# A two-layer decoder trunk on one core: the 512-column products of every dense layer in parts of 256 columns

## The chip, the cores and the metric

The kernel runs on one core of one Trainium2 chip. The metric is the device time of one execution in microseconds. The kernel before takes 604.91 us (median of 3 runs, 603.92 to 605.07).

## The reference, cut to what matters

Two decoder layers (DEPTH = 2) over 256 tokens of width 1024. Each layer is a token mixer and a squared-ReLU MLP, each followed by a residual and a LayerNorm. Layer 0 mixes with stick-breaking attention, layer 1 with block attention, which for 256 tokens is plain causal softmax attention with rotary positions. All inputs are float32.

```python
for i in range(DEPTH):
    h = layer_norm(DEEPNORM_ALPHA * h + mixers[i](h), ln1_g, ln1_b)
    h = layer_norm(DEEPNORM_ALPHA * h + squared_relu_mlp(h, w1, w2), ln2_g, ln2_b)

def stick_breaking_attention(x, w_qkv, w_o):     # block attention has the same two products
    q, k, v = (split_heads(t, SB_HEADS) for t in jnp.split(x @ w_qkv, 3, axis=-1))
    ...
    return merge_blocks(o) @ w_o

def squared_relu_mlp(x, w1, w2):                 # w1 is 1024 x 4096, w2 is 4096 x 1024
    return jnp.square(jax.nn.relu(x @ w1)) @ w2
```

## The kernel before

**Dense products.** Every float32 operand is split into a high part (rounded to the type that TensorE takes at full rate) and a low rest: ScalarE rounds (line 205, `hi`), VectorE subtracts (line 206, `lo`). A product x·w is then three matmuls: high·high, high·low, low·high, all added into one PSUM bank. Weights come by DMA in units of 128 partitions x 4 x 512 (1 MB), are split on chip in halves of 1024 columns, and live in 5 pairs of buffers (`hi`, `lo`).

There are two forms. In `projT` (lines 329 to 349) the weights are the stationary operand and the 256 tokens are the moving one: its matmuls have 256 columns. It makes Q and K of layer 0 (`qkT_ps`) and the hidden layer of the MLP from its third block on (`up_ps` with `xh` or `xl` named first). In `mm3` (lines 193 to 197) the 128 tokens of one half t are stationary and the weights move: its matmuls have 512 columns, a whole bank. `mm3` makes V (`v_ps`), Q and K of layer 1 (`qk_ps`), the output projection (`wo_ps`), the first two hidden blocks of each MLP (`up_ps` with `hi` or `lo` named first, by `up_tok`) and the MLP's second product (`dn_ps`, by `down`). In the trace a name like `dn_ps<-hi,hh` gives the output, the moving operand (weights, `hi` or `lo`) and the stationary one (`hh` or `hl`, high and low of the hidden layer). Every matmul has a weight load of its own (LDWEIGHTS, engine PEld), also where two in a row have the same stationary operand.

**The MLP.** In each layer `up` and `down` alternate: 96 matmuls of 256 columns, then 48 of 512. The last product of the last layer alone already has one bank in two halves (`down`, line 678): 24 matmuls of `dn_ps` with 256 columns.

**The order.** A planner (`Plan`) builds the program. TensorE's dense matmuls are written in a fixed order; attention pieces, transposes, splits and loads are put in where the planner's own clocks say that their inputs are there (`poll` and `wait`). `mm3` advances the planner's TensorE clock by 3 x (0.006 + 0.000435 x columns), 0.686 for 512 columns. So a change of this number can move pieces on all engines. Attention pieces: `qkT` or `qk`, then (layer 1) rotary products on VectorE and an addition on GpSimd (line 543), transposes `tp`, scores `sc` (14 matmuls), softmax or stick-breaking on ScalarE and VectorE, transposes `pt_ps`, a copy (line 498), the product with V `o`.

After each LayerNorm the new x is transposed on TensorE (`xt`), split by ScalarE and VectorE into `xh` and `xl`, and used by the next dense product.

Of the kernel before, what the change touches and what calls it, by code (L numbers as in the profile page):

```python
# [154 lines left out]
def trunk(ctx: ExitStack, tc: tile.TileContext, x, xt, cst, cstb, w, ln, out):  # L155
# [17 lines left out]
    clock = plan.clock  # L173

    def abank(name):
        return acc.tile([P, 512], F32, tag="acc", name=name)
# [13 lines left out]
    def mm(ps, sta, mov, start, stop):  # L190
        nc.tensor.matmul(ps, sta, mov, start=start, stop=stop)  # L191

    def mm3(ps, sh, sl, wh, wl, start, stop):
        mm(ps, sh, wh, start, False)
        mm(ps, sh, wl, False, False)
        mm(ps, sl, wh, False, stop)
        clock["pe"] += 3 * (0.006 + 0.000435 * ps.shape[-1])

    def here():
        return Tok("pe", clock["pe"], 0.2)  # L200
# [24 lines left out]
    def tok(t):  # L225
        return slice(t * P, (t + 1) * P)
# [46 lines left out]
    def retire(n):  # L273
        plan.give([("split", n)], clock["pe"])
# [47 lines left out]
    def proj(t, us, ps):  # L322
        for k in range(KT):
            u = us[k // 4]
            plan.wait([u.tok[k % 4], XT[t][k]])
            mm3(ps, xh[:, k, tok(t)], xl[:, k, tok(t)], u.hi[:, k % 4, :], u.lo[:, k % 4, :], k == 0, k == KT - 1)
        plan.poll()
# [84 lines left out]
    for l in range(DEPTH):  # L412
# [162 lines left out]
        for kind in seq:  # L575
            us = take(2)
            j = int(kind[1])
            if kind[0] == "V":
                for t in range(NT):
                    plan.wait(take=[("acc", 1)])  # L580
                    ps = abank("v_ps")
# [14 lines left out]
        def wo(t, half):  # L596
            oh, ol = OT[half]
            us = (wo0, wo1)[half]
            ready = []
            for n in range(2):  # L600
                for k in range(4):
                    plan.wait([us[n].tok[k], mixed[2 * half + k // 2, k % 2]])
                    mm3(banks[t][n], oh[:, k, tok(t)], ol[:, k, tok(t)], us[n].hi[:, k, :], us[n].lo[:, k, :],
                        half == 0 and k == 0, half == 1 and k == 3)
                ready.append([(0, 512, here())])
            return ready
# [63 lines left out]
        def down(c, t, us):  # L670
            last = c == NFC - 1
            ready = [[], []]
            if not last:
                loop = [(n, k, 0, 512) for k in range(4) for n in range(2)]
            elif l < DEPTH - 1 or t == 0:
                loop = [(n, k, 0, 512) for n in range(2) for k in range(4)]
            else:
                loop = [(n, k, c0, c1) for n, c0, c1 in ((0, 0, 512), (1, 0, 256), (1, 256, 512)) for k in range(4)]
            for n, k, c0, c1 in loop:
                plan.wait([us[n].tok[k], HR[c][t][k]])  # L680
                hh, hl = HT[c]
                mm3(dn[t][n][:, c0:c1], hh[:, k, tok(t)], hl[:, k, tok(t)], us[n].hi[:, k, c0:c1], us[n].lo[:, k, c0:c1],
                    c == 0 and k == 0, last and k == 3 and c1 == 512)
                if k == 3:
                    ready[n].append((c0, c1, here()))
            if t == 1:
                plan.give([("st", 1)], clock["pe"])
                retire(2)
            return ready
# [8 lines left out]
        for c in range(2, NFC):  # L698
            us = take(2)
            up(c, us)  # L700
            retire(2)
            if c == 2:
                plan.wait(take=[("acc", 4)])
                dn = [[abank("dn_ps") for _ in range(2)] for _ in range(NT)]
            us = take(2)
            for t in range(NT):
                down(c - 2, t, us)
        d6, d7 = take(2), take(2)
        ended = []
        for t in range(NT):  # L710
            down(NFC - 2, t, d6)
            r = down(NFC - 1, t, d7)
            end = norm(t, dn[t], r, g2, to_x if l < DEPTH - 1 else to_out, base[t])
            base[t] = end[-1]
            ended += end
# [93 lines left out]
```

## Time and profile before

| | |
|---|---|
| median of 3 runs | 604.91 us (603.92 to 605.07) |
| the profiled execution | 603.84 us |
| its span, first to last instruction | 602.1 us |
| mean granted TensorE clock | 0.995 |
| TensorE matmuls busy | 591.5 us, 98% of the span, 3652 matmuls |
| weight loads busy | 507.1 us, 84% |
| VectorE, ScalarE, GpSimd busy | 389.7, 290.5, 24.6 us |
| DMA | 49% of 16 engines, 109 MB |

How to read it: a matmul's recorded duration (0.28 us for 256 columns, 0.39 us for 512) includes its way through a pipeline and overlaps with the next one. What a matmul costs in a stream is the distance from its start to the next start. That distance, called pace below, is read from the first and the last start of a run of matmuls and their count. The long chain of work through the program lies on TensorE for 95% of the span. The rest of the span is about 8.9 us of loading at its start and 8.2 us of LayerNorm and output at its end.

### The profile page before, as it was taken

What the parts mean: (1) busy time and instruction counts of PE and PEld (TensorE: products, weight loads), DVE (VectorE), ACT (ScalarE), POOL (GpSimd) and SP (SyncE); (2) the same over time, 40 slices, a digit from 0 to 9 for tenths busy, and PEclk for the clock granted to TensorE, in tenths of its full rate; (3) what the DMA queues carried; (4) which work ended last, traced back from release to release, by engine and by line L of the source; (5) the groups of instructions that cost most, each with busy time, mean ns of one, the idle gap of its engine ahead of it and who ended that gap; (6) DMA issues with size and microseconds to landing.
All of it is one profiled execution on the core that took longest, in us unless ns stands there. A gap on an engine that the chain in (4) does not pass through costs nothing.

```text
span 602.1 us, 8790 instructions
## 1 busy us (share of the span) xinstructions
PE 591.5 (98%) x3652; PEld 507.1 (84%) x3652; DVE 389.7 (65%) x492; ACT 290.5 (48%) x419; POOL 24.6 (4%) x30
## 2 busy tenths in 40 slices
PE   8999999999999999999999999999999999999994
PEld 6899987879899899898877777778798998899883
DVE  5877874878455554655879787668667537446454
ACT  5866663436443543642536655626346426435400
POOL 0000000000000000000122022000000000000000
PEclk9999999999999999999999999999999999999998
DMA  8994335185546337337274443443764464365101
GB/s 310 393 334 143 126 154 200 70 277 169 215 179 269 149 143 279 140 144 275 71 249 170 145 144 132 140 141 101 249 260 162 149 270 169 157 235 209 72 0 70
DMA packets 17895, 109.31 MB, mean 182 GB/s; under 512 B 1984, under 2 KB 2624, under 8 KB 5824
## 3 DMA queue, kind: packets, MB, share of 16 engines
q1 hardware_dynamic: 17856, 108.76, 49.0%
q8 instruction: 28, 0.46, 0.3%
q14 instruction: 11, 0.09, 0.0%
HBM read 107.71 MB, written 1.05 MB: 181 GB/s over the span
## 4 chain that ended last, share of the span: by engine, by line
PE 95%; DVE 2%; ACT 1%; DMA 1%; SPq 0%; issue 0%; DVEq 0%; ACTq 0%
PE dn_ps L191 29%; PE up_ps L191 28%; PE wo_ps L191 7%; PE v_ps L191 7%; PE qk_ps L191 7%; PE qkT_ps L191 7%; PE sc L191 3%; PE o L509 2%; PE xt L387 1%; PE tp L556 1%; DMA h<-in_xt 1%; DVE lo L206 1%; DVE xl L206 1%; PE ht_ps L663 1%; PE pt_ps L491 1%; PE pt_ps L493 1%
## 5 line engine op out<-in xcount | busy, mean ns | idle before, releaser
L206 DVE TENSOR_TENSOR lo<-raw,hi 128x1024 fp32r<-128x1024 f32 (+1 forms) x196 | 229.7, 1213 | 48.8 <-ACT hi L205 47.1
L205 ACT CAST hi<-raw 128x1024 fp32r<-128x1024 f32 (+1 forms) x196 | 192.0, 1032 | 64.2 <-issue 42.4
L191 PE MATMUL up_ps<-xh,hi 128*128 128x256 f32 x384 | 106.4, 277 | 0.0
L191 PE MATMUL up_ps<-xl,hi 128*128 128x256 f32 x384 | 106.2, 276 | 0.0
L191 PE MATMUL up_ps<-xh,lo 128*128 128x256 f32 x384 | 106.1, 276 | 0.0
L191 PE MATMUL dn_ps<-hi,hl 128*128 128x512 f32 (+1 forms) x260 | 101.5, 390 | 0.0
L191 PE MATMUL dn_ps<-lo,hh 128*128 128x512 f32 (+1 forms) x260 | 101.0, 388 | 0.0
L191 PE MATMUL dn_ps<-hi,hh 128*128 128x512 f32 (+1 forms) x260 | 100.2, 385 | 0.0
L191 PEld LDWEIGHTS up_ps<-xl,hi 128*128 128x128 f32 x384 | 72.1, 188 | 0.5
L191 PEld LDWEIGHTS up_ps<-xh,hi 128*128 128x128 f32 x384 | 72.1, 188 | 0.5
L630 DVE SCALAR_TENSOR_TENSOR r<-up_ps,r 128x512 f32<-128x512 f32 x32 | 22.0, 688 | 78.0 <-ACT r L628 78.0
L191 PEld LDWEIGHTS up_ps<-xh,lo 128*128 128x128 f32 x384 | 72.2, 188 | 0.0
L628 ACT ACTIVATE r<-up_ps 128x512 f32<-128x512 f32 x32 | 19.1, 596 | 95.0 <-PE up_ps L191 95.0
L191 PEld LDWEIGHTS dn_ps<-lo,hh 128*128 128x128 f32 x260 | 48.8, 188 | 10.5
L191 PEld LDWEIGHTS dn_ps<-hi,hh 128*128 128x128 f32 x260 | 48.8, 188 | 10.0
L191 PEld LDWEIGHTS dn_ps<-hi,hl 128*128 128x128 f32 x260 | 48.9, 188 | 9.4
L191 PE MATMUL qkT_ps<-xh,hi 128*128 128x256 f32 x128 | 36.8, 287 | 0.0
L191 PE MATMUL qkT_ps<-xh,lo 128*128 128x256 f32 x128 | 35.8, 280 | 0.2 <-DVE lo L206 0.2
L191 PE MATMUL qkT_ps<-xl,hi 128*128 128x256 f32 x128 | 35.7, 279 | 0.0
L205 ACT CAST xh<-xt 128x512 fp32r<-128x512 f32 x12 | 7.0, 587 | 42.9 <-PE xt L387 41.1
L191 PE MATMUL v_ps<-hi,xh 128*128 128x512 f32 x64 | 26.4, 413 | 0.0
L191 PE MATMUL qk_ps<-hi,xh 128*128 128x512 f32 x64 | 26.3, 411 | 0.0
(97 smaller groups left out, 885.8 us busy)
## 6 DMA issues: line engine op xcount, KB each, us to landing
raw<-in_w SPq DMA_DIRECT2D x64, 1024.0 KB, 5.0
raw<-in_wqkv SPq DMA_DIRECT2D x22, 1024.0 KB, 5.2
raw<-in_wo SPq DMA_DIRECT2D x8, 1024.0 KB, 4.8
raw<-in_first SPq DMA_DIRECT2D x8, 256.0 KB, 4.8
gb<-in_l_ln_g SPq DMA_DIRECT2D x4, 512.0 KB, 4.0
gb<-in_l_ln_b SPq DMA_DIRECT2D x4, 512.0 KB, 5.8
h<-in_x SPq DMA_DIRECT2D x2, 512.0 KB, 7.7
h<-in_xt SPq DMA_DIRECT2D x3, 256.0 KB, 4.8
```

The costliest lines, as they stand in the source:

```text
L191: nc.tensor.matmul(ps, sta, mov, start=start, stop=stop)
L205: f = lambda: nc.scalar.copy(hi(), src())
L206: g = lambda: nc.vector.tensor_tensor(lo(), src(), hi().bitcast(F32), op=ALU.subtract)
L387: nc.tensor.transpose(XB[t][:, n, k * P:(k + 1) * P], h[t][:, (4 * n + k) * P:(4 * n + k + 1) * P], ident)
L491: nc.tensor.transpose(ps[:, j, 0:P], pj[:, T:T + P], ident)
L493: nc.tensor.transpose(ps[:, j, T:T + P], pj[:, P:T], ident)
L509: nc.tensor.matmul(o[HD * j:HD * j + HD, 0, kt * P:T], v[kt][:, hd * HD:(hd + 1) * HD], pt[:, 0:T] if kt == 0 else pt[:, T:T + P], start=k ...
L556: nc.tensor.transpose(tb["tp"][:, pr, c0:c0 + P], QK[g, t]["qk"][:, e * T + pr * P:e * T + pr * P + P], ident)
L628: nc.scalar.activation(box["r", n], ps, AF.Relu)
L630: return dve(512, lambda: nc.vector.scalar_tensor_tensor(box["r", n], ps, 0.0, box["r", n], op0=ALU.max, op1=ALU.mult), after=[a], rank=0. ...
L663: nc.tensor.transpose(box["ht"][:, 0, k * P:(k + 1) * P], box["r", 0][:, k * P:(k + 1) * P], ident)
```

## The change

`mm3` cuts its columns into parts and runs the three matmuls of one part before those of the next. A part has 256 columns, with one exception: in the last block of `down` in each layer, for the first token half and the second bank, the parts have 384 and 128 columns. The planner's TensorE clock now advances per part by 3 x max(0.113, 0.000435 x columns): 0.678 for 512 columns in two parts of 256, 0.840 for 384 and 128.

```diff
-    def mm3(ps, sh, sl, wh, wl, start, stop):
-        mm(ps, sh, wh, start, False)
-        mm(ps, sh, wl, False, False)
-        mm(ps, sl, wh, False, stop)
-        clock["pe"] += 3 * (0.006 + 0.000435 * ps.shape[-1])
+    def mm3(ps, sh, sl, wh, wl, start, stop, cut=256):
+        n = ps.shape[-1]
+        parts = [slice(a, min(a + cut, n)) for a in range(0, n, cut)]
+        for i, c in enumerate(parts):
+            mm(ps[:, c], sh, wh[:, c], start and i == 0, False)
+            mm(ps[:, c], sh, wl[:, c], False, False)
+            mm(ps[:, c], sl, wh[:, c], False, stop and i == len(parts) - 1)
+            clock["pe"] += 3 * max(0.113, 0.000435 * (c.stop - c.start))
...
                 mm3(dn[t][n][:, c0:c1], hh[:, k, tok(t)], hl[:, k, tok(t)], us[n].hi[:, k, c0:c1], us[n].lo[:, k, c0:c1],
-                    c == 0 and k == 0, last and k == 3 and c1 == 512)
+                    c == 0 and k == 0, last and k == 3 and c1 == 512, 384 if last and t == 0 and n == 1 else 256)
```

On TensorE, at the start of the first `down` of layer 0 (`hi_1445` and `hi_1479` are the weights of the two banks; numbers are buffer names). Before:

```order
L191 MATMUL dn_ps<-hi_1445,hh 128x512
L191 MATMUL dn_ps<-lo_1446,hh 128x512
L191 MATMUL dn_ps<-hi_1445,hl 128x512
L191 MATMUL dn_ps<-hi_1479,hh 128x512
L191 MATMUL dn_ps<-lo_1480,hh 128x512
L191 MATMUL dn_ps<-hi_1479,hl 128x512
```

The same place on TensorE with the change:

```order
L191 MATMUL dn_ps<-hi_1721,hh 128x256
L191 MATMUL dn_ps<-lo_1722,hh 128x256
L191 MATMUL dn_ps<-hi_1721,hl 128x256
L191 MATMUL dn_ps<-hi_1721,hh 128x256
L191 MATMUL dn_ps<-lo_1722,hh 128x256
L191 MATMUL dn_ps<-hi_1721,hl 128x256
L191 MATMUL dn_ps<-hi_1767,hh 128x256
```

Each triple of 512 columns has become two triples of 256; a low weight (`lo`) is asked for after one matmul of 256 columns, not after one of 512.

On TensorE, in the last `down` of layer 0, first token half, where the first bank ends and the second begins, with the change:

```order
L191 MATMUL dn_ps<-lo_3124,hh 128x256
L191 MATMUL dn_ps<-hi_3123,hl 128x256
L191 MATMUL dn_ps<-hi_3200,hh 128x384
L191 MATMUL dn_ps<-lo_3201,hh 128x384
L191 MATMUL dn_ps<-hi_3200,hl 128x384
L191 MATMUL dn_ps<-hi_3200,hh 128x128
L191 MATMUL dn_ps<-lo_3201,hh 128x128
L191 MATMUL dn_ps<-hi_3200,hl 128x128
```

In this bank each of the 4 steps of its loop has three matmuls of 384 and three of 128 columns, where before it had three of 512; so 12 matmuls of 512 per layer, 24 in all, become 24 of 384 and 24 of 128.

On VectorE, in layer 1 behind the first three rotary products (`qk`, `rot`): `lo` is a weight split, `qkl` the split of a transposed head pair, `sma` the row maxima of scores. Before:

```order
L206 TENSOR_TENSOR lo_2909<-raw_2845,hi_2908 128x1024 x2
L206 TENSOR_TENSOR lo_2928<-raw_2871,hi_2927 128x1024
L206 TENSOR_TENSOR qkl<-tp,qkh 128x512
L206 TENSOR_TENSOR lo_2928<-raw_2871,hi_2927 128x1024
L533 TENSOR_TENSOR qk<-qk_ps,const 128x512
L465 TENSOR_REDUCE sma<-sc 128x2 x2
L468 TENSOR_SCALAR sma<-sma 128x4
L538 TENSOR_TENSOR rot<-qk_ps,const 128x512
L206 TENSOR_TENSOR qkl<-tp,qkh 128x512
```

The same place on VectorE with the change (three lines further down in the file):

```order
L209 TENSOR_TENSOR lo_3656<-raw_3553,hi_3655 128x1024 x2
L209 TENSOR_TENSOR lo_3684<-raw_3594,hi_3683 128x1024 x2
L536 TENSOR_TENSOR qk<-qk_ps,const 128x512
L541 TENSOR_TENSOR rot<-qk_ps,const 128x512
L209 TENSOR_TENSOR qkl<-tp,qkh 128x512 x2
L209 TENSOR_TENSOR lo_3747<-raw_3653,hi_3746 128x1024 x2
L468 TENSOR_REDUCE sma<-sc 128x2 x2
L471 TENSOR_SCALAR sma<-sma 128x4
L209 TENSOR_TENSOR qkl<-tp,qkh 128x512 x2
```

The fourth rotary product now stands ahead of the first head pair's split and its first scores; from here to the output projection of layer 1 the attention pieces stand in another order on TensorE, ScalarE and VectorE. In layer 0's attention a few pieces move by one or two steps of the loop, in the MLPs none.

## Rows read from the trace of the kernel before

**Rows 1.** The page: busy time of each engine; granted TensorE clock in 40 slices

```profile
PE 591.5 (98%) x3652; PEld 507.1 (84%) x3652; DVE 389.7 (65%) x492; ACT 290.5 (48%) x419; POOL 24.6 (4%) x30
...
PEclk9999999999999999999999999999999999999998
```

**Rows 2.** Waits of TensorE: line waited for, us in total, times, longest

```profile
PE warm_ps L285 <- POOL keep L451: 1.3, 1, 1.3
...
PE qk_ps L191 <- DVE lo L206: 0.2, 1, 0.2
```

**Rows 3.** Groups by form, TensorE: output, operands, shapes, count | busy, mean ns

```profile
L191 PE MATMUL dn_ps<-hi,hl 128*128 128x512 f32 x252 | 99.3, 394 | 0.0
...
L191 PE MATMUL v_ps<-hi,xh 128*128 128x512 f32 x64 | 26.4, 413 | 0.0
```

**Rows 4.** Timeline of TensorE, last `down`: start us, us, line, operands

```profile
560.81 0.39 PE L191 MATMUL dn_ps<-hi,hh 128*128 128x512 f32 x1
...
590.79 0.39 PE L191 MATMUL dn_ps<-hi,hl 128*128 128x512 f32 x1
591.02 0.28 PE L191 MATMUL dn_ps<-hi,hh 128*128 128x256 f32 x1
...
593.63 0.28 PE L191 MATMUL dn_ps<-hi,hl 128*128 128x256 f32 x1
```

**Rows 5.** Timeline of TensorE, one `up` block: its start, its seventh, its end

```profile
164.69 0.28 PE L191 MATMUL up_ps<-xh,hi 128*128 128x256 f32 x1
...
165.40 0.28 PE L191 MATMUL up_ps<-xh,hi 128*128 128x256 f32 x1
...
175.49 0.28 PE L191 MATMUL up_ps<-xh,lo 128*128 128x256 f32 x1
```

**Rows 6.** Timeline of TensorE, three runs of `qkT` in layer 0's attention

```profile
35.94 0.28 PE L191 MATMUL qkT_ps<-xl,hi 128*128 128x256 f32 x1
...
45.59 0.28 PE L191 MATMUL qkT_ps<-xh,lo 128*128 128x256 f32 x1
...
52.92 0.28 PE L191 MATMUL qkT_ps<-xl,hi 128*128 128x256 f32 x1
...
55.16 0.28 PE L191 MATMUL qkT_ps<-xh,lo 128*128 128x256 f32 x1
...
59.76 0.28 PE L191 MATMUL qkT_ps<-xl,hi 128*128 128x256 f32 x1
...
62.25 0.28 PE L191 MATMUL qkT_ps<-xh,lo 128*128 128x256 f32 x1
```

**Rows 7.** Stretches: us, busy of PE, PEld, DVE, ACT, POOL, clock, DMA, GB/s

```profile
35.94:45.59 9.65, 9.65 (x83) 9.65 (x83) 6.86 (x8) 5.23 (x7) 0.00 (x0) 1.00 0.94 336
165.40:175.49 10.09, 10.09 (x92) 10.09 (x90) 4.57 (x4) 2.76 (x3) 0.00 (x0) 1.00 0.72 274
297.40:397.40 100.00, 99.47 (x577) 76.96 (x576) 78.73 (x135) 57.13 (x123) 16.30 (x9) 1.00 0.49 169
```

**Rows 8.** Timeline of TensorE: transposes of 128 columns, and scores of 128 columns

```profile
394.12 0.27 PE L491 MATMUL pt_ps<-const,p 128*128 128x128 f32 x1
...
395.32 0.27 PE L493 MATMUL pt_ps<-const,p 128*128 128x128 f32 x1
...
76.84 0.23 PE L191 MATMUL sc<-qkh 64*128 64x128 f32 x2
76.89 0.29 PE L191 MATMUL sc<-qkl,qkh 64*128 64x128 f32 x2
77.01 0.28 PE L191 MATMUL sc<-qkh,qkl 64*128 64x128 f32 x2
```

**Rows 9.** Timeline of TensorE where `up` of layer 0 waits for a low weight

```profile
128.12 0.39 PE L191 MATMUL up_ps<-hi,xh 128*128 128x512 f32 x1
128.65 0.51 PE L191 MATMUL up_ps<-lo,xh 128*128 128x512 f32 x1
```

**Rows 10.** Timeline of GpSimd in layer 1's attention: a rotary addition

```profile
316.90 2.12 POOL L543 TENSOR_TENSOR qk<-qk,rot 128x512 f32<-128x512 f32 x1 [2.67 <-DVE rot L538]
```

## The prediction

> **What bounds the kernel now.** [...] The groups by form give the counts: dn_ps has three groups of 252 matmuls with 512 columns, and v_ps, qk_ps, wo_ps and the first up_ps have three of 64 each [rows 3]. That is 756 + 4 x 192 = 1524 matmuls with 512 columns, all of which the change cuts. 24 go to 384 and 128 columns, 1500 to two parts of 256.
>
> **Paces before.** 512 columns: 132 dn_ps matmuls start from 560.81 to 590.79, 29.98 / 131 = 228.85 ns [rows 4]. 256 columns of the very same product: 24 from 591.02 to 593.63, 2.61 / 23 = 113.5 ns [rows 4]. An up block: 90 starts from 165.40 to 175.49, 10.09 / 89 = 113.4 ns [rows 5]. So two parts of 256 take 226.8 ns for 228.85. But there is a second level. In layer 0's attention 83 matmuls of the same shape start from 35.94 to 45.59, 9.65 / 82 = 117.7 ns; from 59.76 to 62.25, 23 matmuls, it is 2.49 / 22 = 113.2 again [rows 6]. The granted clock is 1.00 in the slow stretch and in the fast one alike, DMA is 0.94 in one and 0.72 in the other, and weight loads are busy without a break in both [rows 7]. The first six matmuls of each of the ten full up blocks are on the slow level, too: 164.69 to 165.40, 0.71 / 6 = 118 ns [rows 5]. A run takes its level after a break (scores, transposes, products with V, or a change of width) and mostly keeps it. I find no cause for it. In the 512-column runs the level is not to be seen: their weight loads have time to spare. At 117.7, two parts cost 235.4 ns, 6.5 more than one matmul of 512.
>
> **The change part by part.**
>
> (a) MLP, dn_ps. 756 less 24 is 732. They stand between up blocks, which run at 113.4 after at most six slow steps, ten times of ten. I take 226.8: 732 x (226.8 - 228.85) = -1.5 us.
>
> (b) Everything else, 768 matmuls (v, qk, wo, the first up). These runs are broken up by attention pieces like layer 0's qkT. There, and in the other runs of 256 columns next to such breaks, 120 of some 450 matmuls were on the slow level (three runs of 84, 21 and 15; the first two are in [rows 6], 2.24 / 19 = 117.9 ns in the second), 27%. So a part costs 113.4 + 0.27 x 4.3 = 114.6, two 229.1: 768 x 0.25 = +0.2 us. Bounds: all fast, -1.6; half slow, 768 x (231.1 - 228.85) = +1.7.
>
> (c) The bank in 384 and 128. No row shows either width in a dense product. 384 lies between 256 and 512: 3/4 of 228.85 is 171.6 ns. For 128 the lower bound is half of 113.4, 57 ns; one step between scores of 128 columns takes 0.05 us, but the next ones 0.12 and more, and twelve transposes of 128 columns start from 394.12 to 395.32, 1.20 / 11 = 109 ns [rows 8]. [...] I take 113.4, the pace of 256, since three 128s come in a row: 24 x (171.6 + 113.4 - 228.85) = +1.35 us; at 57 ns it would be 0. [...]
>
> (d) Stalls. In four places the second matmul of a triple waits for a low weight that VectorE finishes just then; one is up of layer 0, whose starts are 0.53 us apart for 0.23 [rows 9], and the same is at 307.93, at 425.74, and less at 16.97. Before, a matmul of 512 ran ahead of the wait; now one of 256 does and its other half comes behind, so that 0.115 us of cover goes each time. Nothing is queued that could fill it: TensorE takes its list in order. With the 0.02 us by which the work ahead is shorter, 4 x 0.13 = +0.5 us. If the low weights came earlier, as VectorE has less than 80% of work there [rows 7], it would be 0.
>
> (e) The new order. Layer 1's attention is reshuffled on three engines. TensorE has 0.53 us not busy in its 100 us [rows 7], so no more than 0.5 us can be gained. Counted in matmuls on the two orders, no distance from scores to their transposes, from these to the product with V, or from transposed heads to scores falls below the shortest of its kind before. The fourth rotary product comes earlier on VectorE, ahead of the transposes that need it; its addition on GpSimd takes 2.12 us [rows 10] and fits behind the 15 matmuls and the scores that stand between (some 4.6 us). I take 0; one addition that came late would cost up to 2.1 us. Layer 0 and the end of the program keep their chains: the last matmuls already have 256 columns.
>
> (f) 1524 more matmuls and loads are more instructions to fetch. Up blocks already run at that rate with no gaps at all, so I take 0.
>
> Sum: -1.5 + 0.2 + 1.35 + 0.5 = +0.55 us on the span of 602.1. The profiled execution took 603.84 with its span and what lies around it; the median of three runs is 604.91. Put on the median: 605.4 us, 0.1% over. A measurement of this kernel can tell 0.2%, 1.2 us, from no change; this is within it.
>
> **The rivals.**
>
> Faster: every run stays on the fast level. Then (b) is -1.6, and the six slow steps at each up block go as well, since no 512 stands ahead of them (10 x 6 x 4.4 ns = 0.26). Sum -1.5 - 1.6 - 0.26 + 1.35 + 0.5 = -1.5, 603.4 us. For it: all ten blocks recover, and 24 parts of the product that is cut were fast [rows 4]. Against it: the long slow run [rows 6]. Cheap parts of 128, (c) near 0, lead to the same side: 604.1 alone, 602.1 with all fast. Together 27%.
>
> Slower: the slow level takes hold in the products that are cut now. The place is (b). Its price is 768 x 8.6 ns = 6.6 us from all fast to all slow, and the sum passes +1.2 us when over 37% of these matmuls are slow (-1.5 - 1.6 + 6.6 s + 1.85 = 1.2). At half it is +2.0, 606.9 us. If a whole MLP of one layer kept it, 366 cut and 480 uncut matmuls would pay 366 x 8.6 + 480 x 4.3 ns = 5.2 us more, 610 us; with ten recoveries that is unlikely. 20%.
>
> Slower, a fixed cost for every matmul: if 1500 more paid a constant, the time would grow with the count. The rows speak against a constant: 2 x 113.4 is less than 228.85 [rows 4, 5]; only the slow level has one, 235.4 - 228.85 = 6.5 ns, +9.8 us if it held everywhere, 616 us. 2%. [...]
>
> Slower, the new order: one rotary addition or weight split late in layer 1, +2.1 us, 607.5. 5%.
>
> **How the numbers follow.** Forecast 46%, faster rivals 27%, slower ones 20 + 2 + 5 = 27%. So faster by over 0.2% 0.27, within 0.46, slower 0.27. The range goes from 602.8 (all fast, and (c) half as dear) to 607.8 (half of (b) slow and a late piece in part); about one in ten is left out on either side. The likeliest case's own range is 603.7 to 606.1.
>
> **What would show it.** In the trace after: dn_ps parts between up blocks at 113 to 114 ns, a dn block at 10.9 us; v, qk, wo and first up parts at 113.4 or 117.7, with the share of the latter; 384s at 172 and 128s at about 113 ns; starts 0.42 us apart at the low-weight waits, with a 256 ahead; no new wait over 0.3 us in layer 1's attention. Parts of 128 near 57 ns, a level of 117.7 through an MLP, or a new wait of a microsecond would prove steps (c), (a) or (e) wrong.

## The result: slower by 1.5%

The changed kernel takes 613.73 us (median of 3 runs, 613.68 to 614.03) for 604.91 before: a ratio of 1.0152, 95% interval 1.0129 to 1.0175. The prediction said 605.4 and no measurable change; the time lies outside its range, by 5.9 us. The profiled execution took 613.68 us, 611.9 of it the span (before 603.84 and 602.1). In the runs beside the experiments below, the kernel before took 604.3 to 604.9.

The page after, its busy times and the granted clock, and the waits of TensorE (line waited for, us in total, times, longest), which answer to [rows 1, 2]:

```profile
PE 601.2 (98%) x5176; PEld 586.1 (96%) x5176; DVE 389.1 (64%) x492; ACT 290.1 (47%) x419; POOL 23.2 (4%) x30
...
PEclk9999999999999999999999999999999999999998
```

```profile
PE warm_ps L288 <- POOL keep L454: 1.3, 1, 1.3
PE up_ps L191 <- DVE lo L209: 0.4, 2, 0.2
PE o L512 <- ACT pt L501: 0.2, 1, 0.2
PE tp L559 <- ACT qkh L208: 0.2, 1, 0.2
...
```

TensorE is still busy for 98% of a longer span, at the same granted clock (0.996, before 0.995). Its waits have grown from 1.9 to 2.5 us in all, and none that is new is longer than 0.2 us. So its matmuls themselves follow one another more slowly. The chain of work that ended last shows where (start, us, engine, output, line, matmuls; a down row holds both token halves, 96 parts). Layer 0's MLP, three rounds and the last run, and wo in two places:

```profile
155.11 10.88 PE dn_ps L191 x96
165.99 11.31 PE up_ps L191 x96
177.30 11.31 PE dn_ps L191 x96
188.61 10.89 PE up_ps L191 x96
199.50 10.88 PE dn_ps L191 x96
210.38 11.31 PE up_ps L191 x96
...
266.08 28.18 PE dn_ps L191 x234
```

```profile
98.44 12.45 PE wo_ps L191 x108
...
112.66 5.66 PE wo_ps L191 x48
```

10.88 us for 96 parts is 113.4 ns each, 11.31 is 117.8: the two spacings of [rows 5, 6]. The level changes each time the work goes from down to up and stays from up to down, in both layers alike; before, all ten full up blocks took 10.91 us and the down pairs 10.98 or 10.99. wo ran fast once (115 ns over its 108 parts) and at 5.66 / 48 = 118 ns elsewhere; v, qk and the first up blocks are at 117.5 to 118 ns nearly throughout. Counted step by step on the timeline (a slow step is 116 to 121 ns; breaks left out), 433 of 540 steps between such parts are slow in layer 0, 843 of 880 in layer 1.

The change of level takes one matmul. The timeline at the switch at 165.8 (start, us, line, operands), 0.11 us apart before it and 0.12 behind it:

```profile
165.49 0.28 PE L191 MATMUL dn_ps<-hi,hh 128*128 128x256 f32 x1
165.60 0.28 PE L191 MATMUL dn_ps<-lo,hh 128*128 128x256 f32 x1
165.71 0.28 PE L191 MATMUL dn_ps<-hi,hl 128*128 128x256 f32 x1
165.82 0.28 PE L191 MATMUL up_ps<-xh,hi 128*128 128x256 f32 x1
165.94 0.28 PE L191 MATMUL up_ps<-xl,hi 128*128 128x256 f32 x1
166.06 0.28 PE L191 MATMUL up_ps<-xh,lo 128*128 128x256 f32 x1
```

By stage, from the first matmul of each on the timeline, the last stage to the recorded end of the last matmul (us; the last three columns are runs told below; "full" up blocks are those in parts of 256 already before):

| stage | before | after | cut_down_only | cut_all_but_down | down_fast |
|---|---|---|---|---|---|
| span's start to the first full up block | 142.28 | 143.60 | 143.59 | 143.99 | 143.28 |
| MLP of layer 0 | 154.94 | 157.93 | 158.01 | 154.87 | 154.33 |
| layer 1 ahead of that point | 142.69 | 145.24 | 142.38 | 145.00 | 142.38 |
| MLP of layer 1 | 153.99 | 157.04 | 157.05 | 153.92 | 153.15 |

The first stage grew by 1.32 us, but 0.63 us of that stand ahead of the first matmul that is cut: v starts at 16.97 us before and at 17.60 after, while the first loads arrive, and this start differs from run to run (16.97 to 18.52 in the traces here). I leave these 0.63 us out. Then 9.3 us = 0.69 + 2.99 + 2.54 + 3.05, for 8.8 between the medians here and 9.1 against the kernel before beside the first experiments.

### The profile page after: what moved, and what is told of

It reads as the page before. It is cut to its first block, busy times and chain, and to the rows that moved or that the text cites. A ratio compares the mean times of both kernels' runs of the same rounds, so it can differ in the third digit from the quotient of the medians.

```text
span 611.9 us, 11835 instructions
## 1 busy us (share of the span) xinstructions
PE 601.2 (98%) x5176; PEld 586.1 (96%) x5176; DVE 389.1 (64%) x492; ACT 290.1 (47%) x419; POOL 23.2 (4%) x30
## 4 chain that ended last, share of the span: by engine, by line
PE 95%; DVE 2%; ACT 1%; DMA 1%; SPq 0%; issue 0%; DVEq 0%; ACTq 0%
PE dn_ps L191 29%; PE up_ps L191 28%; PE wo_ps L191 7%; PE v_ps L191 7%; PE qk_ps L191 7%; PE qkT_ps L191 7%; PE sc L191 3%; PE o L512 2%; PE xt L390 1%; DMA raw<-in_first 1%; DVE lo L209 1%; DVE xl L209 1%; PE tp L559 1%; PE pt_ps L494 1%; PE ht_ps L666 1%; PE pt_ps L496 1%
## 5 line engine op out<-in xcount | busy, mean ns | idle before, releaser
L191 PE MATMUL dn_ps<-hi,hh 128*128 128x256 f32 (+2 forms) x512 | 143.2, 280 | 0.0
L191 PE MATMUL dn_ps<-lo,hh 128*128 128x256 f32 (+2 forms) x512 | 142.7, 279 | 0.0
L191 PE MATMUL dn_ps<-hi,hl 128*128 128x256 f32 (+2 forms) x512 | 142.7, 279 | 0.0
L191 PEld LDWEIGHTS dn_ps<-hi,hl 128*128 128x128 f32 x512 | 96.2, 188 | 0.0
L191 PEld LDWEIGHTS dn_ps<-hi,hh 128*128 128x128 f32 x512 | 96.2, 188 | 0.0
L191 PEld LDWEIGHTS dn_ps<-lo,hh 128*128 128x128 f32 x512 | 96.0, 187 | 0.0
L191 PE MATMUL v_ps<-hi,xh 128*128 128x256 f32 x128 | 37.1, 290 | 0.0
L191 PE MATMUL qk_ps<-hi,xh 128*128 128x256 f32 x128 | 37.0, 289 | 0.0
L191 PE MATMUL up_ps<-hi,xh 128*128 128x256 f32 x128 | 36.6, 286 | 0.0
L191 PE MATMUL wo_ps<-hi,oh 128*128 128x256 f32 x128 | 36.5, 285 | 0.0
```

## The experiments

All edits are to the changed kernel, unless said otherwise. Where a ratio stands, it is to the kernel before on the same chip; a time without one comes from a single run.

**Which part costs what.** cut_down_only and cut_all_but_down:

```
-    def mm3(ps, sh, sl, wh, wl, start, stop, cut=256):
+    def mm3(ps, sh, sl, wh, wl, start, stop, cut=512):      # cut_down_only
...
-     ..., 384 if last and t == 0 and n == 1 else 256)
+     ..., 512)                                              # cut_all_but_down
```

> The kernel before with the cut in down alone (the 384 and 128 parts included); v, qk, wo and the first two up blocks stay at 512. If the stages are independent, the MLPs cost what they cost in the changed kernel, 3.0 us each more than before (0.7 us of each for the 384 and 128 parts, the rest for blocks at 117.8 ns), and the rest costs what it did: 610.9 us. Prediction's own sizes: 604.8 us (-1.5 for the cut, +1.35 for the 384 and 128 parts). If the order of the work or the code's length cost the time, this one stays near 605 us as well.

> The kernel before with the cut in v, qk, wo and the first two up blocks alone; down stays at 512. If the stages are independent: layer 0 ahead of its MLP +1.3 us, layer 1 ahead of its MLP +2.5 us, MLPs as before, 608.8 us, with nearly all of these parts at 117.7 ns. Prediction's own sizes: 605.6 us (27% of the parts slow, +0.2, and four waits, +0.5). If the slow level of these parts is a thing of chance, other runs of parts than in the changed kernel are slow here.

Measured, for 610.9 and 608.8 expected: 610.67 us (1.0099, 1.0084 to 1.0114) and 607.82 us (1.0053, 1.0038 to 1.0068). The table has their stages: each part costs in its own stages about what it costs in the whole change, and the sums agree (6.0 + 3.2 for 9.1). The same blocks are at 117.8 ns as in the changed kernel, with one exception: the first qk run of layer 1, which here stands behind whole products of down and there behind parts at 117.8 ns, is fast here. Changed kernel first, cut_all_but_down second:

```profile
301.69 6.36 PE qk_ps L191 x54
```

```profile
299.03 6.12 PE qk_ps L191 x54
```

That is 113.3 ns a part for 117.8. So what comes before counts for this run too, which stands outside the MLPs. cut_down_only has an order of its own ahead of layer 1's MLP, since a whole product advances the planner's clock by 0.668 there; that stage is 0.3 us shorter for it.

**Is it the waits at the switch?** In up the first two waits stand on matmuls 0 and 2, in down on 0 and 1. up_low_second, in projT for up's call only:

```
-                mm(ps, u.hi[:, kk, cs], xl[:, k, :], False, False)
-                mm(ps, u.lo[:, kk, cs], xh[:, k, :], False, k == KT - 1 and half == 1)
+                mm(ps, u.lo[:, kk, cs], xh[:, k, :], False, False)
+                mm(ps, u.hi[:, kk, cs], xl[:, k, :], False, k == KT - 1 and half == 1)
```

> The changed kernel with one thing moved: in the MLP's up blocks the product with the low weights comes second of its three matmuls instead of third, so that the two first waits of a block stand on its matmuls 0 and 1, as they do in down, and no longer on 0 and 2. In the changed kernel the spacing of the 256-column matmuls goes from 113.4 to 117.8 ns, or back, at every switch from down to up and at none from up to down. Theory W (a wait that stands on the third matmul of a triple shifts the pairs of weight load and matmul): the switch from down to up no longer flips; the whole MLP of a layer keeps the level with which it begins, 607 us if that is the fast one, 619 us if it is the slow one. Theory S (the switch itself flips, because the operands change places: the weight tile is the stationary operand in up and the moving one in down): the up blocks alternate between 10.9 and 11.3 us as now, 613.7 us.

Measured: 613.71 us (1.0148, 1.0131 to 1.0165), the same alternation (up blocks of 10.89 and 11.31 us in its chain). Theory W has fallen.

**Is it the break ahead of the block?** down_ends_whole:

```
-  ... 384 if last and t == 0 and n == 1 else 256)
+  ... 384 if last and t == 0 and n == 1 else 512 if t == 1 and n == 1 and k == 3 else 256)
```

> The changed kernel, but the last of the sixteen products of each 512 hidden columns in down (second token half, second bank, last k) stays one part of 512. In the kernel before every up block that follows a 512-column run has six parts at about 118 ns and then runs at 113.4. Theory of levels (a run takes its level from the break that it follows, and 256-column runs keep it from up to down): every up block comes out at 10.9 us and every down pair behind it at 10.9 us; both MLPs lose the slow blocks, 3.2 us each, and the total is 607 us. Rival (the level is not set by the break, but alternates with something else that goes on, such as the two PSUM buffers that up takes in turn): the alternation of 10.9 and 11.3 us stays, 613.7 us.

Measured: 608.17 us (1.0058, 1.0043 to 1.0073), for 607 expected. Its chain in layer 0's MLP:

```profile
166.30 10.91 PE up_ps L191 x96
177.21 10.88 PE dn_ps L191 x93
188.09 10.91 PE up_ps L191 x96
199.00 10.88 PE dn_ps L191 x93
```

Three whole matmuls ahead of each up block, and every one of them is fast, as are the down pairs that follow. About half of the missing microsecond is in the last down blocks: behind the parts of 384 and 128 they are at 117.8 ns again (in layer 0, 41 matmuls from 286.82 to 291.65 and 40 behind them; in layer 1, 41), which I had counted as fast. At 4.4 ns each that is 0.5 us; the rest I have not traced. So the recoveries that the prediction counted ten times of ten were not the up block's own doing: they came with the whole matmuls ahead of it.

**Does each switch flip?** two_switches takes down's last product over into the next up block, behind its first three matmuls:

```
             for kk, f in loop:
...
                 clock["pe"] += 3 * 0.1175
+                if then:
+                    then()          # the last product of the down ahead
+                    then = None
```

> The changed kernel, but the last product of down ahead of each up block (six matmuls) is issued after the first three matmuls of that up block, so that the work changes twice from down to up and not once. Theory S (each change from down to up moves the spacing to the other level, each change from up to down keeps it): two changes cancel, the MLP of a layer keeps the level with which it begins; that is the fast one in the changed kernel, so up blocks and down blocks come out at 10.9 us each and the total at 607 us. Rival T (the level changes once per up block, whatever stands at the switch, for example with the PSUM buffer that the block takes): 10.9 and 11.3 us go on alternating, 613.7 us. If short runs of three and six matmuls disturb the spacing in a way of their own, neither pattern is seen.

Measured: 608.11 us (1.0062, 1.0047 to 1.0077), for 607 expected; the last down blocks are slow here too, and nine parts or so at each switch.

```profile
164.96 0.36 PE up_ps L191 x3
165.32 0.71 PE dn_ps L191 x6
166.02 10.55 PE up_ps L191 x93
176.58 10.20 PE dn_ps L191 x90
```

The first three matmuls of up, the six of down and the start of the next run are slow (0.71 / 6 = 118 ns), then the block is fast (10.55 / 93 = 113.4), in all ten up blocks alike. Two flips cancel, as theory S has it. So in these two kernels, this one and the changed one, the level changes at the change from down to up, not once per block; and the blocks keep it between.

**Does the place of the operands count?** At such a switch the operands move: in up the weight tile is the stationary operand and xh or xl the moving one, in down the weight tile moves and hh or hl is stationary. In the build, xh and xl begin 96 bytes behind a multiple of 256 in each partition, the hidden tiles (and oh, ol) 96, the weight tiles 160. The gaps in SBUF that the kernel reserves allow xh and xl to be shifted; h and v lie behind them and move with them, all else stays, and so does the order of the work on every engine:

```
-GAP = (224, 288)
+GAP = (32, 480)      # shifted_x; (288, 224) x_higher_64; (160, 352) x_lower_64
...                   # (256, 256) x_higher_32; (352, 160) x_higher_128
```

> The changed kernel with the two unused gaps in SBUF resized from 224 and 288 bytes per partition to 32 and 480, so that xh, xl, h and v lie 192 bytes lower and everything behind them stays. If the level at a switch depends on where the two operands lie against one another, the pattern of slow and fast runs changes (up and down blocks no longer alternate, or other runs of v, qk and wo are slow), and the total with it, by up to 10 us either way. If it does not, 613.7 us and the same blocks slow.

> The changed kernel with xh, xl, h and v 64 bytes higher per partition (gaps of 288 and 224). In the changed kernel's build xh and xl begin 96 bytes behind a multiple of 256, the hidden tiles hh and hl too, the weight tiles 160 behind one; moved down by 192 bytes, xh and xl stood at 160 like the weights, and 6 us were lost. Theory of addresses (what counts is where the stationary and the moving operand of a matmul lie, modulo 256 bytes): 64 bytes up is the same place modulo 256 as 192 bytes down, so the spacing is 120 ns in every up block (11.5 us) and 113.4 ns in every down block up to the 384 and 128 parts, total 619.7 us. Rival (only the distance itself, or the tiles' starts modulo 512 or more): some other pattern.

> The changed kernel with xh, xl, h and v 64 bytes lower (gaps of 160 and 352): xh and xl at 32 behind a multiple of 256, 128 from the weights. Theory of addresses: the up blocks, v and the qk products change their level against the changed kernel, down and wo, which don't read xh, keep 113.4 or 117.8 ns. If 120 ns comes only where both operands lie alike modulo 256, no up block has it here, and the total lies between 603.5 us (all of them fast) and 616 us (all at 117.8 ns); if alike modulo 128 is enough, 619 us as before.

> The changed kernel with xh, xl, h and v 32 bytes higher (gaps of 256 and 256): xh and xl at 128 behind a multiple of 256, 32 from the weights. Theory of addresses: the pattern differs from the changed kernel's; nearer to the weights' place it should be nearer to the 120 ns of like places, so 613.7 to 619.7 us. Rival (what counted was one bad place): the pattern and the 613.7 us of the changed kernel.

> The changed kernel with xh, xl, h and v 128 bytes higher (gaps of 352 and 160): xh and xl at 224 behind a multiple of 256, 64 above the weights where the changed kernel has them 64 below. Theory of addresses with a distance that counts either way: the changed kernel's 613.7 us and its alternating blocks. With a distance that has a sign: another pattern, between 603.5 us (all cut products fast) and 616 us.

And for the other operand, hidden_higher_64 puts 64 bytes ahead of the pool of hh, hl, oh and ol:

```
+    pool("gap", 1).tile([P, 16], F32, tag="gap64", name="gap64")
     st = pool("st", 3)
```

> The changed kernel with a gap of 64 bytes per partition ahead of the pool that holds the hidden tiles hh and hl and the attention outputs oh and ol, so that these, the stationary operands of down and wo, lie like the weight tiles modulo 256 bytes; xh and xl stay. Theory of addresses for both operands: down and wo run at 120 ns (a pair of down blocks 11.5 us), while v, the qk products and the first two up blocks, which read nothing that moved, stay at 117.7 ns. If only the place of xh and xl counts: 613.7 us and the changed kernel's pattern.

| run | xh, xl | hidden | weights | full up block | down pair | total, us |
|---|---|---|---|---|---|---|
| changed kernel | 96 | 96 | 160 | 10.89 and 11.31 | 10.88 and 11.31 | 613.73 |
| shifted_x | 160 | 96 | 160 | 11.52 | 10.88 | 619.71 (1.0254, 1.0236 to 1.0271) |
| x_higher_64 | 160 | 96 | 160 | 11.52 | 10.88 | 619.53 |
| x_lower_64 | 32 | 96 | 160 | 11.39 | 11.30, 11.31 | 622.57 |
| x_higher_32 | 128 | 96 | 160 | 11.36 | 11.30, one in five 10.88 | 619.75 |
| x_higher_128 | 224 | 96 | 160 | 11.31 | 11.31 | 617.40 |
| hidden_higher_64 | 96 | 160 | 160 | 10.90 | 11.50 | 618.11 |

(Columns two to four are the places modulo 256 bytes, by the build's allocation; blocks in us, slow starts of a block included.) Chains of shifted_x, of x_higher_64 and of hidden_higher_64, in layer 0's MLP:

```profile
169.65 11.52 PE up_ps L191 x96
181.16 10.88 PE dn_ps L191 x96
```

```profile
169.39 11.52 PE up_ps L191 x96
180.90 10.88 PE dn_ps L191 x96
```

```profile
156.56 11.50 PE dn_ps L192 x96
168.06 10.90 PE up_ps L192 x96
178.96 11.50 PE dn_ps L192 x96
```

192 bytes down and 64 bytes up give the same blocks to 0.01 us, though the two places are 256 bytes apart: between these two places only the remainder by 256 counts. The remainder by 128 is not enough: x_lower_64 and x_higher_64 are 128 bytes apart, and an up block took 11.39 us in one and 11.52 in the other. Where the stationary and the moving operand had the same remainder, a 256-column part took 11.5 / 96 = 120 ns, in either pair: in up when xh moved onto the weights' remainder (shifted_x, x_higher_64), in down when the hidden tiles did (hidden_higher_64). (Both times the common remainder was 160; no run has two operands alike at another one.) In hidden_higher_64 the products that read nothing that moved had mostly their old spacing, but not all: the first up run of each layer, which follows wo, took 6.12 us for 6.36, and no full up block was slow any more. The alternation of up blocks is seen at the changed kernel's places alone; in all six shifted runs every full up block of a run has one and the same spacing. The misses: in x_lower_64 I expected at most 619 us, and got 622.57, since not only up came to 118.7 ns but down, which reads nothing that moved, stayed on 117.8 throughout, for 113.4 in x_higher_64 with the hidden tiles at the same place: what comes before a block still counts. x_higher_128 came out at 617.4 for at most 616: its v runs became mostly fast (rows below: 3.42 / 30 = 114 ns for 3.54 / 30 = 118 in the changed kernel), but the MLPs were slow throughout, with down, which reads nothing that moved, among them. In x_higher_32 nearness was not the measure: at 32 bytes from the weights an up part took 118.3 ns, at 128 bytes, in x_lower_64, 118.7, and the total of 619.75 comes from four down pairs in five that stayed slow. Changed kernel first, x_higher_128 second:

```profile
388.94 3.54 PE v_ps L191 x30
```

```profile
391.13 3.42 PE v_ps L191 x30
```

**Do whole products hide it?** whole_x_higher_64 is the kernel before with the gaps of x_higher_64:

> The kernel before with xh, xl, h and v 64 bytes higher, the place at which every 256-column product that reads them took 120 ns. The up blocks and the qk products of layer 0, which were in parts of 256 already, should go to 120 ns (an up block from 10.9 to 11.5 us, twelve of them, +7.4 us; the qk products of layer 0 +2 us). Open is what the whole products of v, qk of layer 1 and the first up blocks do: if a 512-column matmul hides the effect, they keep 229 to 230 ns and the total is 614 us; if not, they go to 240 ns and the total is 618 us.

Measured: 612.83 us, beside 604.32, for 614 expected.

```profile
156.36 10.99 PE dn_ps L191 x48
167.35 11.52 PE up_ps L191 x96
...
420.61 6.14 PE up_ps L191 x27
```

The up blocks, in parts of 256 in this kernel too, go from 10.91 to 11.52 us. The whole products, of the first up blocks among them, stay at 6.14 / 27 = 227 ns at the place where two halves took 240 (6.48 us for 54 in x_higher_64). So at this place the whole products of these blocks do not show what two parts of each show: 227 ns beside 240.

**Would a whole product at the head of each run bring the fast level outside the MLPs?** first_whole is cut_all_but_down with 512 for k == 0 in proj and wo:

> The kernel with the cut in v, qk, wo and the first two up blocks alone (607.8 us in the run before), but the first of the products of each bank (k = 0) stays one part of 512, so that each run of 256-column parts begins behind three whole matmuls. If a whole product is what brings the fast level (as in down), these runs come out at 113.4 ns and the total near 604 us; if what counts is the operands of the run behind it, and a run whose stationary operand is xh or oh falls to 117.8 ns again, 607.5 us.

Measured: 607.56 us (1.0054, 1.0039 to 1.0069), for 607.82 without: no. A wo run of 48 parts' work took 5.64 us for 5.65. Two runs that were fast without the whole product are slow behind it, the first qk run of layer 1 (6.12 us above) and the long wo run of layer 0 (12.45 us in cut_all_but_down):

```profile
298.86 6.33 PE qk_ps L191 x48
```

```profile
98.22 12.84 PE wo_ps L191 x96
```

The whole product is no cure in itself. Behind whole products of down the parts in up and in this qk run were fast (10.91 us in down_ends_whole, 6.12 in cut_all_but_down); behind whole products of qk and wo they were not (6.33 and 12.84 us). What makes the difference, these runs do not show.

**The order, and a version that is faster than both.** order_alone is the kernel before with the planner's new cost; down_fast cuts in down only, ends each second token half whole and has no 384 and 128; down_fast_old_order is the same with the planner's old cost.

```
-        clock["pe"] += 3 * (0.006 + 0.000435 * ps.shape[-1])
+        clock["pe"] += 3 * 0.113 * (ps.shape[-1] // 256)         # order_alone
...
-    def mm3(ps, sh, sl, wh, wl, start, stop, cut=256):
+    def mm3(ps, sh, sl, wh, wl, start, stop, cut=512):           # down_fast
...
-     ..., 384 if last and t == 0 and n == 1 else 256)
+     ..., 512 if t == 1 and n == 1 and k == 3 else 256)          # down_fast
```

> The kernel before with the changed kernel's cost in the planner (0.113 us for each 256 columns) and whole products: TensorE, VectorE, ScalarE and GpSimd take the changed kernel's order, and nothing is cut. Theory: the order costs nothing that counts, as step (e) of the prediction has it, and the loss comes from the spacing of the parts alone: between 604.1 and 604.9 us. Rival: the order costs some of the 2.5 us that layer 1 loses ahead of its MLP, 605.5 us or more.

> The cut in down alone, without the 384 and 128 parts, and with the last product of the second token half left whole as in the run before. Theory of levels: both MLPs run at the fast level up to the last two down blocks, each pair of down blocks 0.1 us shorter than with whole products: some 0.6 us for each layer, 603.5 us, just under the kernel before. Rival (what the cut takes from the matmuls in down comes back as waiting or at the slow level behind the transposes in the last block): 604.6 us or more.

> The cut in down alone, with the last product of the second token half left whole and no parts of 384 and 128, as in the run at 602.7 us, but with the planner's costs and so the order of the kernel before. If the gain of that run came from the spacing in the MLPs (0.6 and 0.8 us in its trace), it stays: 603.0 us. If it came from the order that went with it (0.3 us in layer 1 ahead of the MLP), less of it: 604 us or more.

Measured: order_alone 604.16 us (0.9996, 0.9988 to 1.0005): the order is worth nothing either way. It is the changed kernel's on all engines, and the stages are 142.66, 154.94, 142.65 and 153.93 us, as before to 0.4 us in the first and 0.1 in the others. down_fast, which shares the order of cut_down_only, 602.73 us (0.9973, 0.9963 to 0.9983) and with the old order 602.74 (0.9972, 0.9960 to 0.9983): the gain is the cut's. Both are a little under the 603.0 and 603.5 expected. The chain of down_fast in layer 0's MLP:

```profile
187.55 10.91 PE up_ps L191 x96
198.46 10.88 PE dn_ps L191 x93
```

## Why the prediction was wrong, step by step

The sum was +0.55 us; the stages give +9.3. Of the 8.7 that are missing, 6.2 are in (a) and 2.5 in (b) with (d).

**(a), the step that failed first.** It took 113.4 ns for every part in down, "ten times of ten", from up blocks that follow whole matmuls [rows 5], and moved that to a program in which no whole matmul is left to follow. (The 24 fast parts of down in [rows 4] stood behind whole matmuls, too.) Forecast -1.5 us; the MLPs grew by 6.0, of which 1.3 are (c), so +4.7. It is made up of six up blocks at 11.31 for 10.91 (+2.4), four down pairs at 11.31 for 10.98 (+1.3), six at 10.88 (-0.6), the run of the last three down blocks, 132 and 120 matmuls at some 7 ns more (+1.9), and the first full up block of each layer (-0.2): together 4.8, near the 4.7. The rival of a slow MLP stood in the text, at 610 us, and was called unlikely for the same ten recoveries. down_ends_whole shows what they were worth: put back three matmuls of 512 ahead of each up block, and all full up blocks recover.

**(b), failed in the same way.** 27% of parts slow was read from runs of 256 columns beside breaks, most of them layer 0's qk products, which have the weight tile stationary. (In these alone it was more, 134 of 355 steps.) The products that are cut have xh or oh stationary, and of their steps 80% are slow in layer 0 and 96% in layer 1. In layer 1 480 such matmuls cost 2.54 us, 5.3 ns each. That is less than the 6.5 that separate two slow parts from a whole matmul; runs of one product between two breaks took 0.70 us before and 0.71 after, so they hardly paid. The last run of wo, 48 parts, took 5.66 us, 118 ns each. So the share was carried over from other runs and was wrong, and the price of 6.5 ns is an upper bound; 3.2 us (0.69 in the first stage and 2.54) stand against +0.7 for (b) and (d).

**(c) held as a sum.** The bank in 384 and 128, six starts of one product and the next:

```profile
286.53 0.39 PE L191 MATMUL dn_ps<-hi,hh 128*128 128x384 f32 x1
286.75 0.34 PE L191 MATMUL dn_ps<-lo,hh 128*128 128x384 f32 x1
286.93 0.34 PE L191 MATMUL dn_ps<-hi,hl 128*128 128x384 f32 x1
287.10 0.22 PE L191 MATMUL dn_ps<-hi,hh 128*128 128x128 f32 x1
287.16 0.28 PE L191 MATMUL dn_ps<-lo,hh 128*128 128x128 f32 x1
287.27 0.28 PE L191 MATMUL dn_ps<-hi,hl 128*128 128x128 f32 x1
287.39 0.39 PE L191 MATMUL dn_ps<-hi,hh 128*128 128x384 f32 x1
```

0.86 us for 3 x 0.229 = 0.69: +0.17 for six of the eight products, +0.13 for the first in each layer, 1.3 us for 1.35. The two widths are off in opposite ways, so that the sum came out in part by luck: the steps of the 128s are 0.06, 0.11 and 0.12 for 0.113 each, those of the 384s 0.22, 0.18 and 0.17 for 0.172. No run shows the 113.4 ns that the sum takes for each 128, as the first one took 0.06. What holds the second and the third at 0.11 and 0.12, the runs do not show either: the weight loads that start between 287.11 and 287.44 are 0.10 to 0.12 us apart as well, with 0.19 us recorded for each.

**(d), too large.** The stall that answers to [rows 9]:

```profile
129.11 0.28 PE L191 MATMUL up_ps<-hi,xh 128*128 128x256 f32 x1
129.57 0.39 PE L191 MATMUL up_ps<-lo,xh 128*128 128x256 f32 x1 [0.18 <-DVE lo L209]
129.80 0.28 PE L191 MATMUL up_ps<-hi,xl 128*128 128x256 f32 x1
```

0.46 and 0.23 us for two steps of 0.118 is a loss of 0.45; before it was 0.53 and, up to the start at 128.99, 0.34 for two of 0.229, 0.41. So 0.04 us at this place, not 0.13: the matmul behind the wait had paid before as well. The third matmul of the triple reads no low weight, and in both traces it starts behind the one that waits, at 128.99 before and at 129.80 here: nothing filled the wait.

**(e) held**: order_alone is at 0.9996. **(f) held**: where the cut parts are fast they follow one another at 113.4 ns, as up blocks did before, so more instructions alone cost nothing that shows.

The rival of a constant for every matmul (2%) had nearly the right total, 616 us, for a wrong reason: it would charge every matmul alike, but the same shape runs at 113.4, 117.8 and 120 ns, by place and by what came before. And the sentence "I find no cause for it" should have moved the chances: with a level that is worth 10 us in the whole program and that nothing in the profile explained, 2 and 20% for its taking hold were too few.

**What stays open.** In the changed kernel, with xh, xl and hidden tiles at 96 and weights at 160, one and the same pair of operands runs at 113.4 or at 117.8 ns, and keeps the level that it has; a switch from down to up turns it, one from up to down does not. At the other places tried this alternation is not seen. Waits at the switch are excluded (up_low_second), one switch as the unit is shown (two_switches), but not what in the engine or the memory carries the level on, nor what it is that repeats with 256 bytes, nor whether weight loads have a part in it (in the 512-column run of [rows 4] they were busy for 24.60 of 29.98 us). The runs that shift tiles also give the products new neighbours in time at new levels, so a block's spacing there is place and history together; the 120 ns of like remainders came out in every full block, behind fast parts (x_higher_64) and behind whole products (whole_x_higher_64, 11.50 to 11.52 us) alike.

## What to carry to other kernels

Take the spacing of matmuls from starts on the timeline, for each pair of operands and for each kind of run ahead of it, and don't move a spacing from one pair to another: here 4.4 ns, seen as a curiosity, were worth most of the 1.5%. With parts of 256 columns the place of stationary and moving tiles in SBUF became a parameter of this kernel: five shifts of xh and one of the hidden tiles moved it from 613.7 to between 617.4 and 622.6 us. None of them helped, but the cut can't be judged apart from the places at which it was tried; judge it by stage. Cut only where the short parts keep the fast spacing: in down alone, with one whole product before each switch and no parts of 384 and 128, the same idea is 0.3% faster than the kernel before.

## What the runs showed of the hardware that I had not expected

All of it is measured, in the runs named.

- 256-column products took 113.4 or 117.8 ns from start to start (changed kernel), 118.3 (up in x_higher_32), 118.7 (up in x_lower_64) or 120 (up in shifted_x and x_higher_64, down in hidden_higher_64), as means of a block, at a granted clock of 0.996 or 0.997. They differed with where both operands lie in SBUF and with what ran before; shifts of -192 bytes (shifted_x) and +64 (x_higher_64) gave the same blocks, 11.52 and 10.88 us.
- With the same remainder by 256 bytes of the stationary and the moving operand, a part took 120 ns, in up (xh on the weights' remainder, 160, in shifted_x and x_higher_64) and in down (hidden tiles on it, in hidden_higher_64).
- Matmuls of 512 columns did not show this: 227 ns in the first up blocks of whole_x_higher_64, at a place where a part of 256 columns took 120 in x_higher_64.
- The kernel before depends on its gaps too: xh and xl 64 bytes higher (whole_x_higher_64), and it took 612.83 us for 604.32.
